# Attention reciprocals spread by GpSimd between two bias steps, and bias tables built a few steps a unit

## The chip, the cores and the metric

The kernel runs on one core of a Trainium2 chip. The core has engines with a queue each: TensorE (PE, matrix products and transposes into PSUM; its weight loads are listed as PEld), VectorE (DVE), ScalarE (ACT), GpSimd (POOL) and SyncE (SP, which issues DMAs). ACT and POOL issue DMAs too. Each engine takes its own instructions in order and waits on semaphores for the others. The metric is the time of one execution in microseconds on the device, lower is better. The time before is the median of three runs, 1032.79 us (1032.4 to 1032.83).

## The reference

One layer of a diffusion trunk: a modulated RMSNorm, a projection into a pooling mixer and into queries, keys and values, neighbourhood attention, an output projection with a gated residual, and a squared-ReLU MLP. The change lies in the neighbourhood attention. Its core, for one row of the 16 x 64 grid of tokens:

```python
s_loc = jnp.einsum('bnqhd,brnkhd->bhnqrk', q_r, k_b).astype(jnp.float32) * scale
bias = rpb[:, dr_idx[None, None, :, None], dc_idx]
s_loc = jnp.where(col_mask, s_loc + bias.astype(jnp.float32), -jnp.inf)
s_ctx = jnp.einsum('bnqhd,bkhd->bhnqk', q_r, k_ctx).astype(jnp.float32) * scale
s = jnp.concatenate([s_loc.reshape(B, H, NA_NCB, NA_QB, n_loc), s_ctx], axis=-1)
p = jax.nn.softmax(s, axis=-1).astype(v.dtype)
```

followed by the weighted sum of the values of the window and of the 256 context keys. There are 8 heads of 64 channels and 1024 queries.

## The kernel before

The kernel computes all of attention in float32. It cuts the 1024 queries into 8 tiles `m` of 128 (16 rows by 8 columns) and the 8 heads into 4 pairs `j`. One pair of heads on one tile is a **unit**; there are 32, numbered `i = 8j + m`. An inner unit has 640 keys a head (three tiles of the grid and the context), an edge unit (m = 0 or 7) 512.

The loop `for i in range(N + 4)` (L1160) is a software pipeline. In iteration i, besides other work:

- `scores(i)` (L969): PE multiplies queries and keys of both heads into two PSUM tiles `S` of two banks each, of which the pool holds two, so the next unit's scores of a head need the tile that this unit's bias step of that head has read. Then, for e = 0 and 1, DVE runs the **bias step** (L998): it adds the bias table `tab` to `S`, writes `sp` and takes the minimum `nm`.
- `turn(i-2)` (L1018): PE transposes, first the reciprocals `rb` of unit i-2 (into small areas of the banks `pa` and `pz`), then the probabilities `sp`. `fifth_kept` (ACT) and `turn_kept` (ACT for one half, DVE for the other, L1045) copy the results out of PSUM.
- `exps(i, e)` (L1003): ACT takes the exponential and its sum `su`.
- `share(i-1)` (L1009): DVE takes the reciprocal of the two sums (`ri`, 128 x 2) and copies it out to `rb` (128 x 128, each reciprocal 64 times), so that the transposes can turn it.
- `values(i-3)` (L1048): PE multiplies probabilities and values into `pa`.
- `weighed(i-4)` (L1065), at the head of the iteration: DVE multiplies `pa` by the turned reciprocals into `f` (L1070).

On PE the order in an iteration is scores, transposes, values. On DVE it is `weighed`, the two bias steps, the copy of the transposes, the reciprocal, the copy to `rb`.

**Tables.** `tables(j)` (L867) builds the bias tables of pair j: two DMAs on SP bring `U` (shifted rows of the bias), and twelve POOL instructions (L883), three for each head and each of two masks, subtract it from the mask into `tab`. There are two sets of table pages, used in turn. In the loop `tables(j+1)` is called as a whole in the iteration of m = 2.

**Order.** The orders of PE, ACT, DVE and SP in the loop are those of the program text (`in_order`, L104), and so is POOL's (`first_pool`, L1149). POOL's share of the loop before the change is: the table steps; adds by DMA (`add_to`, L187) in iterations 1 and 2 (`y<-y`), at i % 8 == 3 (`y<-f`, `ss<-f`, behind `weighed`), at i % 8 == 7 (`f<-ss`, which must wait for `ss<-f` to land) and at i = 32 (`to_0w`, `to_1w`); and three small reductions over the partitions for the modulation. Of these `mod_out` (L250) in iteration 4 writes a row to DRAM in four DMAs (`ga`); `column_sums` (L619) in iterations 5 (`sc`) and 8 (`sh`) does the same and then reads that row back by a further DMA on POOL's queue:

```python
def column_sums(name, acc, to, bank):
    nc.scalar.copy(acc[:, :256], mod_sums_of(name, acc, bank))
    mod_out(name, acc)
    nc.gpsimd.dma_start(to, gates[name].rearrange("o (k p) -> p (o k)", p=P))
```

In the text of an iteration these stand ahead of `scores(i)`.

Of the kernel before, what the change touches and what calls it, by code (L numbers as in the profile page):

```python
# [80 lines left out]
def hybrid_block(ctx, tc, x, ctx_in, w_mod, b_mod, gp1, gp2, w_in, pool_w, rpb, w_out, w1, w2, vectors,  # L81
                 mask, edge, out):
    nc = tc.nc
# [12 lines left out]
    def sm(name, n, bufs=1):  # L96
        return small.tile([P, n], F32, tag=name.split("_")[0], name=name, bufs=bufs)

    def page(name, dt=F32):
        return act.tile([P, 1024], dt, tag="pg", name=name)  # L100


    @contextmanager
    def in_order(*engines):  # L104
        block = nc.cur_bb
        n = len(block.bb.instructions)
        last = {}
        yield last
        assert nc.cur_bb is block
        for i in block.bb.instructions[n:]:  # L110
            if i.engine in engines:
                if i.engine in last:
                    tc.add_manual_dep(i, last[i.engine].name,
                                      mybir.DependencyInfo(mybir.DependencyClass.NoSync, mybir.DependencyReason.DATA),
                                      reason="order")
                last[i.engine] = i
# [154 lines left out]
    with tc.tile_pool(name="ps1", bufs=6, space=PSUM) as ps1, tc.tile_pool(name="tmp1", bufs=3) as tmp:  # L271

        def bank(name):
            if name[:2] == "pm" or name in ("pxt1_0", "pxt0_2", "pxt1_7", "pct2", "pct3"):
                return lasting(name)
            return ps1.tile([P, 512], F32, tag="mm", name=name)
# [488 lines left out]
        def token_raw(name):  # L765
            raw = [tmp.tile([P, 512], F32, tag="t", name=f"{name}r{i}", bufs=7) for i in range(4)]
            for i in range(4):
                nc.sync.dma_start(raw[i], stored[name][:, i])
            return raw

        def token_operand(name, raw):
            rows_of[name] = []
            for i in range(4):
                h = page(f"{name}h{i}", F32R)
                split(raw[i], h[:, :512], h[:, 512:])
                rows_of[name].append((h[:, :512], h[:, 512:]))
                yield
# [39 lines left out]
        def use(step):  # L817
            for _, put, i in islice(uses, len(plan[step + 1]) if step + 1 < len(plan) else 0):
                put(i)
                fetch()  # L820
# [46 lines left out]
        def tables(j):  # L867
            if j < 2:
                tabs.append([page(f"tab{j}{e}") for e in range(2)])
                for t in tabs[j]:  # L870
                    nc.gpsimd.memset(t[:, NLOC:NKEY], 0.0)
            u = wraw.tile([P, 1024], F32, tag="raw", name="U0w") if j == 0 else page(f"U{j}")
            u = u.rearrange("p (e t) -> p e t", e=2)
            for e in range(2):
                base = rpb.offset + (2 * j + e) * TR * TC
                nc.sync.dma_start(u[:, e, :ULEN], bass.AP(tensor=rpb.tensor, offset=base,
                                                                 ap=[[TC, QR], [1, QC], [1, ULEN]]))
            for e in range(2):
                uv = u[:, e, : QR * TC].rearrange("p (r c) -> p r c", c=TC)
                t = tabs[j % 2][e]  # L880
                for a, o in ((1, 0), (0, NKEY)):
                    for i in range(3):
                        nc.gpsimd.tensor_tensor(  # L883
                            t[:, o + i * P : o + (i + 1) * P].rearrange("p (r c) -> p r c", c=QC),
                            msk[0][:, a, i], uv[:, :, i * QC : (i + 1) * QC], sub)


        kT, qT = [None] * 4, [[None] * 2 for _ in range(4)]
# [36 lines left out]
        def half_product(name, of, j, banks):  # L925
            a, w = operand[name]
            seventh(banks[j], j, a, weights[w, of], name not in ("P2", "P3", "P4"))
# [3 lines left out]
        with in_order(ET.PE, ET.Pool, ET.Activation, ET.DVE, ET.SP) as pooling:  # L931
            banks = {of: [bank(f"p{of}{j}") for j in range(2)] for of in "KQ"}
            use(-1)
            for step, (n, of, j) in enumerate([(n, of, j) for n, of in products for j in range(2)]):
                half_product(n, of, j, banks[of])
                use(step)
                if step in (5, 9, 17):
                    name = {5: "S1", 9: "S4", 17: "S3"}[step]
                    parts = token_operand(name, sraw[name])
                if step in (5, 7, 9, 11, 17, 19):  # L940
                    next(parts)
                    next(parts)
                if step in (7, 11):
                    name = {7: "S4", 11: "S3"}[step]
                    sraw[name] = token_raw(name)
                if step == 14:
                    mask_page()
                if step == 20:
                    tables(0)
                if step in (21, 22):  # L950
                    for g in range(2):
                        pool_mixed(2 * (step - 21) + g)
                kept_product(n, of, j, banks[of][j])


    with (
# [5 lines left out]
        units = [(j, m) for j in range(4) for m in range(NM)]  # L962
        probs, least, sums, shares, turns, turned, fifths, heads = {}, {}, {}, {}, {}, {}, {}, {}
# [5 lines left out]
        def scores(i):  # L969
            j, m = units[i]  # L970
            inner = 0 < m < NM - 1
            n = NKEY if inner else 4 * P
            o = 1 if m == 0 else 0
            q = qT[j][m // 4]
            cols = slice((m % 4) * P, (m % 4 + 1) * P)
            heads = [slice(e * HD, (e + 1) * HD) for e in range(2)]
            S = [ps_s.tile([P, 1024], F32, tag="S", name=f"S{j}_{m}_{e}") for e in range(2)]
            if inner:
                parts = ((128, kT[j][:, (m - 1) * P : (m + 2) * P]), (512, kc[:, j, :]))
            else:  # L980
                parts = ((0, kc[:, j, :]), (256, kT[j][:, (m + o - 1) * P : (m + o + 1) * P]))
            for c0, keys in parts:
                for e, hs in enumerate(heads):
                    nc.tensor.matmul(S[e][:, c0 : c0 + keys.shape[1]], q[hs, cols], keys[hs], start=True, stop=True)  # L984
            halves = lambda a: a.rearrange("p (a b) -> p a b", a=2)
            for e in range(2):
                t = tabs[j % 2][e]
                sp = att.tile([P, NKEY], F32, tag="sp", name=f"sp{j}_{m}_{e}", bufs=6)[:, :n]
                if inner:
                    s, bt, to = S[e][:, 128:768], t[:, :NKEY], sp  # L990
                else:
                    s, to = halves(S[e][:, 0:512]), halves(sp)
                    if o:
                        bt = halves(t[:, 2 * P : 8 * P])[:, :, P:]
                    else:
                        bt = halves(t[:, NLOC : NLOC + 512])
                nm = sm(f"nm_{i}_{e}", 1, 6)
                nc.vector.tensor_tensor_reduce(out=to, in0=s, in1=bt, scale=1.0, scalar=BIG, op0=add, op1=ALU.min,  # L998
                                               accum_out=nm)
                probs[i, e] = sp  # L1000
                least[i, e] = nm

        def exps(i, e):  # L1003
            if e == 0:
# [2 lines left out]
            nc.scalar.activation(sp, sp, AF.Exp, bias=least[i, e], scale=-1.0, accum_out=sums[i][:, e : e + 1])  # L1007

        def share(i):  # L1009
            ri = sm(f"ri_{i}", 2, 2)  # L1010
            nc.vector.reciprocal(ri, sums[i])
            shares[i] = att.tile([P, P], F32, tag="ri", name=f"rb{i}", bufs=2)
            nc.vector.tensor_copy(shares[i].rearrange("p (e t) -> p e t", e=2),
                                  ri.rearrange("p (e o) -> p e o", o=1).to_broadcast([P, 2, HD]))


# [56 lines left out]
        N = len(units)  # L1073
# [78 lines left out]
        with in_order(ET.PE, ET.Activation, ET.DVE, ET.SP) as projected:  # L1152

            def last_query(n, j):
                half_product(n, "Q", j, last_queries)
                kept_product(n, "Q", j, last_queries[j])

            for j in range(2):
                last_query("P7", j)
            for i in range(N + 4):  # L1160
                if i < N and units[i][1] == 2 and units[i][0] < 3:
                    tables(units[i][0] + 1)
                if i in LOADS:
                    weight_load(0, kks[LOADS.index(i)])
                if i == N:
# [44 lines left out]
                else:  # L1210

                    t = i - N
# [17 lines left out]
                    turn_kept(i - 2, 1, nc.vector.tensor_copy)  # L1230
                if i < 2:
                    last_query("P4", i)
                if 0 < i <= N:
                    share(i - 1)
                if 2 < i <= N + 2:
                    values(i - 3)
# [754 lines left out]
```

## Time and profile before

| | |
|---|---|
| median of 3 runs | 1032.79 us |
| profiled execution, its own span | 1030.8 us |
| attention stage in it | 218.8 to 322.4 us |
| DMA in it | 222.68 MB, mean 216 GB/s |

The profile is of one execution. Its page gives the busy time of each engine (share of the span, number of instructions), and the chain of work that ended last, followed back from the end, by engine. Other views list the instructions in order of time (start, duration, engine, line, operation, `out<-in`, shapes, count, and in brackets the idle time before and what ended it); who waited for whom (total us, times, longest); groups of instructions by line (busy us, mean ns of one, idle before); DMA issues (KB each, median us from issue to landing); and the busy time of PE, PEld, DVE, ACT and POOL in a stretch, followed by the granted TensorE clock (1.00 is full), the DMA share and GB/s. Ends of matmuls are modelled.

### The profile page before, as it was taken

How to read it: one execution, taken by the hardware profiler on the slowest of the kernel's cores; microseconds unless marked ns; L12 is line 12 of the kernel's file. 1: busy time of each engine (PE TensorE's matmuls, PEld its weight loads, DVE VectorE, ACT ScalarE, POOL GpSimd, SP SyncE). 2: the span in 40 equal slices, each digit the busy share in tenths (PEclk: the TensorE clock that was granted, in tenths of full speed). 3: DMA queues.
4: the chain of work that ended last, by engine and by line, in shares of the span. 5: the costliest groups of instructions: out<-in, count | busy, mean ns of one | idle time of the engine just before them, and what ended most of it. 6: DMA issues, size and time to landing. Idle time of an engine off the chain costs nothing.

```text
span 1030.8 us, 15588 instructions
## 1 busy us (share of the span) xinstructions
PE 1017.8 (99%) x5782; PEld 834.2 (81%) x5782; DVE 751.8 (73%) x1187; ACT 543.7 (53%) x941; POOL 110.7 (11%) x168
## 2 busy tenths in 40 slices
PE   8999999999999999999999999999999999999997
PEld 6788888877887888888888888888888888888885
DVE  5588767858996587878998887855766666547576
ACT  7573255328887556776655544555543334334431
POOL 3011200244311311310000000000000000000001
PEclk9999999999999999999999999999999999999999
DMA  9999798632337866795786666637967766555556
GB/s 343 332 255 338 246 265 296 204 86 80 72 95 194 203 180 200 253 237 168 267 269 210 204 210 214 205 122 241 327 220 271 248 226 220 202 180 189 176 182 211
DMA packets 123132, 222.68 MB, mean 216 GB/s; under 512 B 9456, under 2 KB 55152, under 8 KB 123056
## 3 DMA queue, kind: packets, MB, share of 16 engines
q1 hardware_dynamic: 96560, 171.14, 50.4%
q0 software_dynamic: 9360, 19.58, 9.5%
q10 hardware_dynamic: 17136, 30.97, 8.0%
q8 instruction: 45, 0.74, 0.3%
q14 instruction: 31, 0.25, 0.1%
HBM read 168.16 MB, written 52.45 MB: 214 GB/s over the span
## 4 chain that ended last, share of the span: by engine, by line
PE 95%; DMA 2%; ACT 1%; DVE 1%; issue 0%; SPq 0%; DVEq 0%; POOLq 0%; ACTq 0%
PE pu L449 4%; PE S L984 4%; PE pa L1060 3%; PE phv L198 3%; PE phz L198 3%; PE phx L198 3%; PE pyx L198 3%; PE phx L200 3%; PE phv L199 3%; PE phx L199 3%; PE pyx L199 3%; PE pyx L200 3%; PE pyv L199 3%; PE pyv L198 3%; PE pyz L199 3%; PE pyz L198 3%
## 5 line engine op out<-in xcount | busy, mean ns | idle before, releaser
L1007 ACT ACTIVATE sp<-sp,nm 128x640 f32<-128x640 f32 (+1 forms) x64 | 51.4, 803 | 20.0 <-DVE nm L998 19.6
L1577 ACT ACTIVATE c<-c 128x512 f32<-128x512 f32 x48 | 30.3, 632 | 47.0 <-DVE c L1697 28.2
L146 ACT CAST wpS<-S 128x512 fp32r<-128x512 f32 x64 | 38.7, 616 | 26.4 <-PE phv L200 9.2
L198 PE MATMUL phx<-thB,wpA 128*128 128x512 f32 x128 | 50.2, 392 | 0.0
L200 PE MATMUL phx<-thB,wpA 128*128 128x512 f32 x128 | 49.8, 389 | 0.0
L199 PE MATMUL phx<-tlB,wpA 128*128 128x512 f32 x128 | 49.8, 389 | 0.0
L152 DVE TENSOR_TENSOR wpS<-S,wpS 128x512 fp32r<-128x512 f32 x64 | 43.4, 685 | 8.3 <-ACT wpS L146 8.3
L998 DVE CUSTOM_DVE_ANT_0 sp<-S,tab 128x640 f32<-128x640 f32 (+1 forms) x56 | 42.9, 803 | 8.8 <-PE S L984 7.3
L1578 ACT ACTIVATE c<-c 128x512 f32<-128x512 f32 x48 | 30.3, 631 | 15.1 <-DVE sa L1660 12.3
L140 POOL TENSOR_TENSOR ry<-vy,nhalf 128x1 f32<-128x1 f32 x8 | 5.9, 740 | 280.7 <-DVE vy L138 280.7
L198 PEld LDWEIGHTS phx<-thB,wpA 128*128 128x128 f32 x128 | 24.0, 188 | 5.5 <-ACT s L1628 0.5
L984 PE MATMUL S<-kT,q 64*128 64x384 f32 (+1 forms) x128 | 27.9, 495 | 0.3 <-DVE nm L998 0.3
L200 PEld LDWEIGHTS phx<-thB,wpA 128*128 128x128 f32 x128 | 24.0, 188 | 5.0
L199 PEld LDWEIGHTS phx<-tlB,wpA 128*128 128x128 f32 x128 | 24.0, 188 | 4.9
L1060 PE MATMUL pa<-pt,v 128*64 128x128 f32 x352 | 25.9, 279 | 0.6 <-ACT px L1040 0.2
L1045 DVE COPY pt<-T 128x512 f32<-128x512 f32 x32 | 22.0, 686 | 5.5 <-PE T L1026 5.5
L198 PE MATMUL phv<-thT,wpA 128*128 128x512 f32 x64 | 25.1, 392 | 0.0
L198 PE MATMUL phz<-thB,wpS 128*128 128x512 f32 x64 | 25.0, 391 | 0.0
L200 PE MATMUL phv<-thT,wpA 128*128 128x512 f32 x64 | 24.9, 389 | 0.0
L199 PE MATMUL phv<-tlT,wpA 128*128 128x512 f32 x64 | 24.9, 389 | 0.0
L200 PE MATMUL phz<-thB,wpS 128*128 128x512 f32 x64 | 24.9, 389 | 0.0
L199 PE MATMUL phz<-tlB,wpS 128*128 128x512 f32 x64 | 24.9, 389 | 0.0
(1100 smaller groups left out, 3359.7 us busy)
## 6 DMA issues: line engine op xcount, KB each, us to landing
b<-in_w SPq DMA_DIRECT2D x64, 512.0 KB, 4.2
hrS<-hdS SPq DMA_DIRECT2D x32, 512.0 KB, 5.1
hrA<-hdA SPq DMA_DIRECT2D x24, 512.0 KB, 5.5
wm<-in_w_mod SPq DMA_DIRECT2D x16, 512.0 KB, 9.7
wa_0w<-in_w SPq DMA_DIRECT2D x16, 512.0 KB, 5.3
wa_1w<-in_w SPq DMA_DIRECT2D x16, 512.0 KB, 4.5
hdA<-c ACTq DMA_DIRECT2D x32, 256.0 KB, 2.8
hdS<-sa ACTq DMA_DIRECT2D x32, 256.0 KB, 2.7
```

The source lines that it names most:

```text
L146: nc.scalar.copy(hi, src)
L152: nc.vector.tensor_tensor(lo, src, hi.bitcast(F32), sub)
L198: nc.tensor.matmul(ps, ahi, bhi, start=first, stop=False, skip_group_check=more)
L199: nc.tensor.matmul(ps, ahi, blo, start=False, stop=False, skip_group_check=more)
L200: nc.tensor.matmul(ps, alo, bhi, start=False, stop=last, skip_group_check=more)
L449: nc.tensor.matmul(pus[b][j], wk(wgt, k, low, j * P, P), r, start=(k == 0 and n == 0), stop=(k == KT - 1 and n == 2))
L984: nc.tensor.matmul(S[e][:, c0 : c0 + keys.shape[1]], q[hs, cols], keys[hs], start=True, stop=True)
L998: nc.vector.tensor_tensor_reduce(out=to, in0=s, in1=bt, scale=1.0, scalar=BIG, op0=add, op1=ALU.min, accum_out=nm)
L1007: nc.scalar.activation(sp, sp, AF.Exp, bias=least[i, e], scale=-1.0, accum_out=sums[i][:, e : e + 1])
L1060: nc.tensor.matmul(pa[e * HD : (e + 1) * HD, cols], v[:, f : f + HD], turns[i][:, e, c] if c < 4 else fifths[i][:, :, (e + 1) * HD : (e + ...
L1577: nc.scalar.activation(r, src, AF.Relu)
L1578: nc.scalar.activation(r, r, AF.Square)
```

## The change

The copy of the reciprocals to `rb` goes from DVE to POOL. The reciprocal and this copy of unit i-1 are issued inside `scores(i)`, between the two bias steps of unit i, instead of near the end of iteration i; only the last unit's stay at the old place. `ri` gets three buffers instead of two. `tables` becomes a generator: its first step (pages, fills, the DMAs of U) runs in the iteration of m = 1, and then three POOL instructions follow in each of the iterations of m = 2 to 5. The tables of the first pair, ahead of the loop, are still built at one go.

```diff
@@ tables(j)
                 nc.sync.dma_start(u[:, e, :ULEN], bass.AP(tensor=rpb.tensor, offset=base,
                                                                  ap=[[TC, QR], [1, QC], [1, ULEN]]))
+            yield
             for e in range(2):
...
                             msk[0][:, a, i], uv[:, :, i * QC : (i + 1) * QC], sub)
+                    yield
@@ ahead of the loop
                 if step == 20:
-                    tables(0)
+                    for _ in tables(0):
+                        pass
@@ scores(i), after the bias step of head e
                 least[i, e] = nm
+                if e == 0 and i > 0:
+                    share(i - 1)
@@ share(i)
-            ri = sm(f"ri_{i}", 2, 2)
+            ri = sm(f"ri_{i}", 2, 3)
             nc.vector.reciprocal(ri, sums[i])
             shares[i] = att.tile([P, P], F32, tag="ri", name=f"rb{i}", bufs=2)
-            nc.vector.tensor_copy(shares[i].rearrange("p (e t) -> p e t", e=2),
+            nc.gpsimd.tensor_copy(shares[i].rearrange("p (e t) -> p e t", e=2),
                                   ri.rearrange("p (e o) -> p e o", o=1).to_broadcast([P, 2, HD]))
@@ the loop
+            coming_tables = iter(())
             for i in range(N + 4):
-                if i < N and units[i][1] == 2 and units[i][0] < 3:
-                    tables(units[i][0] + 1)
+                if i < N and units[i][1] == 1 and units[i][0] < 3:
+                    coming_tables = tables(units[i][0] + 1)
+                next(coming_tables, None)
...
-                if 0 < i <= N:
+                if i == N:
                     share(i - 1)
```

## The prediction

> **What bounds the kernel now.** I read the page from the top: busy times, then the chain that ended last, then, for the attention stage where all edits lie, the stretch's busy times.
>
> ```profile
> span 1030.8 us, 15588 instructions
> PE 1017.8 (99%) x5782; PEld 834.2 (81%) x5782; DVE 751.8 (73%) x1187; ACT 543.7 (53%) x941; POOL 110.7 (11%) x168
> ...
> PE 95%; DMA 2%; ACT 1%; DVE 1%; issue 0%; SPq 0%; DVEq 0%; POOLq 0%; ACTq 0%
> ```
>
> ```profile
> 218.80:322.40 103.60, 102.88 (x1490) 81.71 (x1489) 87.88 (x258) 85.11 (x225) 34.92 (x63) 1.00 0.44 111
> ```
>
> PE is 95% of the chain, and in the attention stage (218.8 to 322.4) it is busy for 102.88 of 103.6 us, against DVE's 87.88. Its ends are modelled, so I check one unit in the timeline: unit 6, whose scores begin at 240.58.
>
> ```profile
> 240.58 0.30 PEld L984 LDWEIGHTS S<-kT,q 64*128 64x128 f32 x4 [0.17 <-DVE nm L998]
> ...
> 241.33 0.60 PE L984 MATMUL S<-kcT,q 64*128 64x256 f32 x4
> 241.54 0.14 PEld L1026 LDWEIGHTS pa<-ident,rb 64*128 64x128 f32 x1
> ...
> 241.96 0.82 DVE L998 CUSTOM_DVE_ANT_0 sp<-S,tab 128x640 f32<-128x640 f32 x1 [0.48 <-PE S L984]
> ...
> 242.71 0.82 DVE L998 CUSTOM_DVE_ANT_0 sp<-S,tab 128x640 f32<-128x640 f32 x1
> ...
> 243.45 0.08 DVE L998 DVE_READ_ACCUMULATOR2_ANT nm<- 128x1 f32 x1
> 243.45 0.69 DVE L1045 COPY pt<-T 128x512 f32<-128x512 f32 x1
> ...
> 243.77 0.30 PEld L984 LDWEIGHTS S<-kcT,q 64*128 64x128 f32 x4 [0.17 <-issue]
> ...
> 244.05 0.15 DVE L1011 RECIPROCAL ri<-su 128x2 f32<-128x2 f32 x1
> ...
> 244.24 0.23 DVE L1013 COPY rb<-ri 128x128 f32<-128x128 f32 x1
> 244.38 0.28 DVE L1070 TENSOR_TENSOR f<-pa,px 128x128 f32<-128x128 f32 x1
> ...
> 244.72 0.14 PEld L1026 LDWEIGHTS pa<-ident,rb 64*128 64x128 f32 x1 [0.22 <-DVE f L1070]
> ```
>
> The unit lasts 243.77 - 240.58 = 3.19 us. PE goes scores, transposes (the one of rb first), values, next scores, with a pause of 0.17 that has no releaser. DVE stands idle 0.48 for S. So PE sets the pace. DVE is what PE sometimes waits for, in a small sum:
>
> ```profile
> PEld S L984 <- DVE nm L998: 2.4, 11, 0.5
> ...
> PEld pa L1026 <- DVE f L1070: 1.6, 7, 0.4
> ```
>
> **The change, part by part.** (a) *The copy leaves DVE*: 0.23 us a unit for 31 of 32 units, as L1013's row has it. DVE has slack in a steady unit, so the saving reaches PE only where the transposes wait for f (L1070): at most 1.6 us.
>
> (b) *The reciprocal moves between the two bias steps.* The second one ends 0.15 later (L1011). The next unit's scores of head 1 reuse the bank it reads. It now ends with its accumulator read at 243.45 + 0.08 = 243.53; PE starts the next scores at 243.77. With 0.15 it is 243.68, still inside, so the price is nothing; the cover is PE's own values, and without that cover it is 0.15 a unit. Where units are shorter than this one (after an edge unit, which has fewer keys) the bank is late already, and there part of (a) is given back. Bounds for (a) and (b) together: a gain of 1.6, a loss of 0.15 x 11 = 1.7 (the 11 waits on nm). I take a gain of 0.5: the 0.15 fits in most units, and of seven waits for f I let about a third go.
>
> (c) *The copy on POOL.* It is not in this trace. The nearest POOL rows, by size, are two at 128x128, a fill-like select and the two-input table step:
>
> ```profile
> masks.py:199 POOL TENSOR_SCALAR_AFFINE_SELECT ident<-ident 128x128 f32<-128x128 f32 x1 | 0.3, 288 | 0.0
> L883 POOL TENSOR_TENSOR tab<-msk,U 128x128 f32<-128x128 f32 x36 | 15.3, 459 | 17.2 <-DMA U<-in_rpb 17.2
> ```
>
> I take 0.28 (one input, as the select), bounds 0.2 and 0.46, and 0.06 for the signal to PE. The reciprocal now ends near 242.71 + 0.15 and rb is wanted at 244.72, behind the next unit's scores. So by itself the copy is hidden, with over 1 us to spare.
>
> (d) *What stands ahead of it on POOL.* This is the part that decides. POOL's order in the loop is written out, so each copy stands behind everything that its iteration puts on POOL before the scores, the DMAs with their waits included:
>
> ```profile
> 238.68 1.91 POOL L253 DMA_DIRECT2D gsc<-accsc  x4 [2.17 <-ACT accsc L621]
> 242.22 0.93 POOL L623 DMA_DIRECT2D sc<-gsc  x1 [1.63 <-DMA gsc<-accsc]
> 248.28 1.95 POOL L253 DMA_DIRECT2D gsh<-accsh  x4 [5.14 <-ACT accsh L621]
> 253.14 0.92 POOL L623 DMA_DIRECT2D s<-gsh  x1 [2.91 <-DMA gsh<-accsh]
> 254.08 4.94 POOL L883 TENSOR_TENSOR tab<-msk,U 128x128 f32<-128x128 f32 x12
> ```
>
> `column_sums` (iterations 5 and 8) sends a row to DRAM and reads it back, and POOL stands still until the row has landed. That the queue really holds later work is in the last row: the table steps of iteration 10 begin at 254.08, just as the DMA of iteration 8 ends, though their U was issued at 244.98 and lands in 3.8:
>
> ```profile
> 244.98 1.25 SPq L876 DMA_DIRECT2D U<-in_rpb  x2
> ```
>
> ```profile
> U<-in_rpb SPq DMA_DIRECT2D x2, 244.5 KB, 3.8
> ```
>
> Today nobody waits for POOL there. After the change rb of unit 4 comes behind the sc DMA (242.22 + 0.93 = 243.15) and rb of unit 7 behind the sh DMA (253.14 + 0.92 = 254.06). Unit 4's transposes stand at 241.54 today, unit 7's here:
>
> ```profile
> 251.32 0.14 PEld L1026 LDWEIGHTS pa<-ident,rb 64*128 64x128 f32 x1
> ```
>
> So PE stands for 243.15 + 0.02 + 0.28 + 0.06 - 241.54 = 1.97 us in iteration 6, and 254.06 + 0.36 - 251.32 = 3.10 us in iteration 9: 5.07 us. PE takes its queue in order, so values and the next scores move by as much, and the stage has no slack to win it back.
>
> (e) *The rest of POOL's queue*:
>
> ```profile
> 308.07 0.85 POOL L188 DMA_DIRECT2D y<-f  x1 [17.59 <-DVE f L1070]
> 308.61 1.19 POOL L188 DMA_DIRECT2D ss<-f  x1
> 317.33 0.86 POOL L188 DMA_DIRECT2D f<-ss  x1 [7.54 <-DMA ss<-f]
> 317.87 1.57 POOL L188 DMA_DIRECT2D to_0w<-in_w_out  x1
> 318.58 2.10 POOL L188 DMA_DIRECT2D to_1w<-in_w_out  x1
> ```
>
> ```profile
> to_1w<-in_w_out POOLq DMA_DIRECT2D x1, 512.0 KB, 13.1
> ```
>
> ```profile
> L146 ACT CAST to_0h<-to_0w x1: 1052/1052/1052, 340.6 to 340.6; 128x1024 fp32r<-128x1024 f32 x1
> ```
>
> At i = 11, 19, 27 two adds stand ahead of the copy: f is ready 0.9 us into the unit (244.66 against 243.77), their issue takes 309.80 - 308.07 = 1.73, the copy 0.34, so rb is there after 3.0; it is wanted after 4.1 (3.19 + 0.95). The table steps, three a unit, take 3 x 0.44 = 1.3 us behind the previous copy: hidden. U is issued one unit sooner and must now be there at m = 2; by the rows above it lands some 4 us before POOL could begin. The tables are whole three units ahead of their first use. The ss<-f wait now stands four units behind its issue, and the longest landing (317.33 - 308.61 = 8.7 us) is shorter than four units (12.8). The adds to t1 (317.87, 318.58) go behind the last copies, about 4 us later; at 13.1 to landing the second is there near 336, and its first reader comes after 340.6. All of (e): nothing, with a loss of 0.5 us as the bound.
>
> (f) *PE's clock.* A pause of PE can cost more than its length. The granted clock at the start and the end of the run:
>
> ```profile
> 1.60:5.20 3.60, 3.60 (x17) 3.60 (x18) 0.35 (x4) 1.21 (x3) 0.00 (x0) 1.00 0.89 306
> 5.20:6.90 1.70, 1.65 (x15) 1.41 (x13) 0.86 (x6) 1.70 (x3) 0.53 (x1) 1.00 1.03 422
> 1020.00:1023.60 3.60, 3.57 (x16) 2.63 (x14) 1.12 (x1) 0.00 (x0) 0.00 (x0) 1.00 0.66 171
> 1023.60:1025.80 2.20, 0.00 (x0) 0.00 (x0) 1.35 (x3) 0.69 (x2) 0.55 (x1) 1.00 0.30 119
> 1025.80:1030.80 5.00, 0.00 (x0) 0.00 (x0) 0.83 (x2) 0.00 (x0) 0.00 (x0) 0.50 0.35 105
> ```
>
> The clock (third number from the right) falls to 0.50 some 2.2 us after the last matmul. At the start 17 matmuls take 3.60 us (0.21 each) and then 15 take 1.65 (0.11 each): half speed for 3.6 us of work before the full one. In iteration 6 PE is empty from about 241.93 (241.33 + 0.60) to 243.51, 1.6 us: under 2.2, the clock stays. In iteration 9 it is empty as far behind the transposes' place (241.93 - 241.54 = 0.39), from 251.71 to 254.42, 2.7 us: over 2.2, so I count one stretch at half clock, which does in 3.6 us the work of 1.8 and costs about 1.7; bounds 0 and 3.6 (both pauses).
>
> The Trainium skill ("TensorE: Matmul & The Clock Gate", section "Part 1: The HAM clock gate (the "warmup" mystery)") asks for a whole idle window of about 3.4 us before the clock is halved, in windows that run freely. By that neither pause is long enough and the sum goes without this term. The trace halved after 2.2 us, which differs, so the row decides here.
>
> **The sum**: -0.5 + 1.97 + 3.10 + 1.7 = +6.3 us. Against the profiled execution's span, 1030.8 + 6.3 = 1037.1; the median of the runs shown, 1032.79, lies 2.0 above that span, so 1039.1.
>
> **Rivals.**
> 1. *The pauses come, the clock stays*: the sum without (f), +4.6, 1037.4. For it: 2.7 us is not much over the 2.2 that were seen, once, at the end of the run. Against it: that one case. The rule of the Trainium skill quoted in (f) speaks for it as well.
> 2. *Both pauses halve the clock*: +8.0, 1040.8. The first pause is 0.6 us short of the 2.2.
> 3. *The bank of head 1 sets the next scores*, if its release needs more than the 0.09 us that (b) leaves (243.77 - 243.68): up to 0.15 in each of 24 inner units, 3.6 on top of the forecast, 1042.7. Against it: the pause ahead of the scores is 0.17 with and without nm as its releaser.
> 4. *Faster: DVE, not PE, paces the stage*, PE's busy time being modelled. Then each unit is shorter by the whole copy, 32 x 0.23 = 7.3 us, against the pauses of 5.1: -2.2, 1030.6. It decides if DVE has no real idle time; against it are the 0.48 us idle before L998 and 87.88 of 103.6.
> 5. *The copies aren't held by the DMA waits* (the change's own order differs from what I read): only the 0.5 of (a), 1032.3, at best 1031.2. Against it: the 254.08 row.
>
> **How the numbers follow.** Forecast 0.43, rival 1 0.28, rival 2 0.11, rival 3 0.06, rival 4 0.06, rival 5 0.06. The range holds the forecast, rivals 1 and 2 (0.82): from rival 1 with the full gain of (a) and (b), 1.1 less, and a landing half a us sooner, 1035.8, to rival 2 with half a us for (e), 1041.3. A measurement of this kernel tells about 0.2% (2.1 us) from no change. Slower by more: the forecast and rivals 1 to 3, 0.88, and a bit is taken off for landings that come much sooner than here: 0.87. Rival 4 and the better end of rival 5 are faster, 0.07; the rest, 0.06, is the same.
>
> **What would show it.** Right: in the changed profile PE's transposes wait for the rb copy on POOL, about 2.0 and 3.1 us, in two units, nowhere else for long; the two copies start at the end of the sc and s reads; the waits for f are below 1.6; the granted clock dips once, after the second pause. Rival 3 shows as S waiting for nm in most units, rival 4 as units below 3.19 us. Wrong altogether: copies that start right after their reciprocal while the sc read is still waiting.

## The result, and the profile after

The changed kernel takes 1037.57 us (median of 5 runs, 1036.74 to 1038.1) against 1032.62 (1032.09 to 1032.83) for the kernel before on the same chip: a ratio of 1.0047, 95% interval 1.0034 to 1.0059. It is 4.95 us slower, inside the forecast range and 1.5 us under the forecast. It lies close to the first rival's number (1037.4): the pauses came, the half clock did not. How far that number was luck is said further down.

The head of the page of the changed kernel:

```profile
span 1035.6 us, 15717 instructions
PE 1018.5 (98%) x5782; PEld 836.1 (81%) x5782; DVE 745.2 (72%) x1155; ACT 544.3 (53%) x941; POOL 120.8 (12%) x200
```

DVE lost 6.6 us of work, POOL gained 10, and PE's work is the same while its share fell: PE waits. For what, the view of waits over the attention stage says (total us, times, longest):

```profile
PEld pa L1031 <- POOL rb L1018: 4.5, 2, 2.4
...
PE pa L1031 <- POOL rb L1018: 3.7, 2, 2.0
```

Two waits of the transposes for rb (PEld and PE list the same two). Before, the waits for f (L1070, now L1075) were seven and made 1.6 us; they are gone from this list, and PE pays two long ones in their place. Where they lie shows in POOL's instructions in order of time:

```profile
239.09 1.95 POOL L253 DMA_DIRECT2D gsc<-accsc  x4 [0.64 <-ACT accsc L621]
242.67 0.94 POOL L623 DMA_DIRECT2D sc<-gsc  x1 [1.63 <-PE S L987]
243.60 0.53 POOL L1018 COPY rb<-ri 128x128 f32<-128x128 f32 x2
...
250.54 1.93 POOL L253 DMA_DIRECT2D gsh<-accsh  x4 [2.12 <-ACT accsh L621]
254.67 0.93 POOL L623 DMA_DIRECT2D s<-gsh  x1 [2.19 <-DMA gsh<-accsh]
255.59 0.53 POOL L1018 COPY rb<-ri 128x128 f32<-128x128 f32 x2
```

Each time the copy starts in the moment in which the read-back's issue ends (242.67 + 0.94; 254.67 + 0.93), and two copies come out together: the late one and the next unit's, which was ready too. (The first wait is put down to PE S by the view; the read follows its row's landing, as in the kernel before, where the idle time was 1.63 as well and the view named the DMA.) PE in iterations 6 and 9:

```profile
240.98 0.30 PEld L987 LDWEIGHTS S<-kT,q 64*128 64x128 f32 x4 [0.17 <-DVE nm L1001]
...
243.96 0.14 PEld L1031 LDWEIGHTS pa<-ident,rb 64*128 64x128 f32 x1 [2.03 <-POOL rb L1018]
```

```profile
252.57 0.30 PEld L987 LDWEIGHTS S<-kT,q 64*128 64x128 f32 x4 [0.17 <-issue]
...
255.94 0.14 PEld L1031 LDWEIGHTS pa<-ident,rb 64*128 64x128 f32 x1 [2.43 <-POOL rb L1018]
```

Without the wait the transposes follow the scores by 0.97 (251.32 against 250.35 before). So the places of the transposes are 240.98 + 0.97 = 241.95 and 252.57 + 0.97 = 253.54, and PE lost 243.96 - 241.95 = 2.0 us and 255.94 - 253.54 = 2.4.

To compare all runs I use one length, called the **loop** below: from the first weight load of unit 0's scores to that of unit 31's, read from the instruction list of each profile. It was 319.27 - 218.83 = 100.44 us before and is 323.51 - 219.18 = 104.33 now, 3.9 more. Units 6 and 9 grew by 1.85 and 2.25 (3.20 to 5.05; 3.07 to 5.32), the other 29 periods together shrank by 0.2. Of the 4.8 us between the two spans the remaining 0.9 lie outside the loop, 0.35 ahead of it and 0.5 behind; they come up again below.

### The profile page after: what moved, and what is told of

Read it like the earlier page. It is cut to its first block, busy times and chain, and to the rows that moved or that the text cites. A ratio compares the mean times of both kernels' runs of the same rounds, so it can differ in the third digit from the quotient of the medians.

```text
span 1035.6 us, 15717 instructions
## 1 busy us (share of the span) xinstructions
PE 1018.5 (98%) x5782; PEld 836.1 (81%) x5782; DVE 745.2 (72%) x1155; ACT 544.3 (53%) x941; POOL 120.8 (12%) x200
## 4 chain that ended last, share of the span: by engine, by line
PE 93%; DMA 3%; ACT 2%; issue 1%; DVE 1%; SPq 0%; POOL 0%; POOLq 0%; DVEq 0%; ACTq 0%
PE pu L449 4%; PE S L987 3%; PE pa L1065 3%; PE phz L198 3%; PE phv L198 3%; PE phx L198 3%; PE pyx L198 3%; PE pyv L200 3%; PE phz L199 3%; PE phv L199 3%; PE pyz L200 3%; PE phx L199 3%; PE phx L200 3%; PE pyx L200 3%; PE pyv L198 3%; PE pyz L198 3%
## 5 line engine op out<-in xcount | busy, mean ns | idle before, releaser
L198 PE MATMUL phz<-thB,wpS 128*128 128x512 f32 x64 | 25.0, 391 | 0.0
L198 PE MATMUL phy<-thT,wpS 128*128 128x512 f32 x64 | 24.9, 389 | 0.0
```

Source lines behind the costliest of these rows:

```text
L198: nc.tensor.matmul(ps, ahi, bhi, start=first, stop=False, skip_group_check=more)
```

## The experiments

My theory: each copy waits on POOL's queue for the DMA waits ahead of it, and this is all of the loss. The rivals: the place between the bias steps costs in every unit; POOL and DVE get in each other's way; the tables in steps cost something.

### The read-backs moved away

```diff
 def column_sums(name, acc, to, bank):
     nc.scalar.copy(acc[:, :256], mod_sums_of(name, acc, bank))
     mod_out(name, acc)
-    nc.gpsimd.dma_start(to, gates[name].rearrange("o (k p) -> p (o k)", p=P))
+
+def read_back(name, to):
+    nc.gpsimd.dma_start(to, gates[name].rearrange("o (k p) -> p (o k)", p=P))
@@ the loop
+                if i == 7:
+                    read_back("sc", scale2)
+                if i == 10:
+                    read_back("sh", s2)
```

> The changed kernel, but the two DMAs on POOL that read the reduced rows back (sc, sh) are issued two iterations later (7 and 10), when their rows have long landed. Theory (copies held behind DMA waits): the transposes' two waits for rb, 2.0 and 2.4 us, go, so 1037.6 - 4.1 = 1033.5 us; if the 0.8 us that PE loses near 360 us also comes from the stalls, 1032.7. Rival (the bank of head 1, or port sharing between POOL and DVE, costs a little in every unit): the time stays above 1036.5.

Measured: 1033.03 us against 1033.03 before on that chip, ratio 0.9999 (0.9991 to 1.0008); loop 100.24. POOL's instructions in this run:

```profile
239.26 1.96 POOL L253 DMA_DIRECT2D gsc<-accsc  x4 [0.64 <-ACT accsc L621]
241.21 0.30 POOL L1020 COPY rb<-ri 128x128 f32<-128x128 f32 x1
243.60 0.29 POOL L1020 COPY rb<-ri 128x128 f32<-128x128 f32 x1 [2.09 <-DVE ri L1018]
244.25 0.94 POOL L625 DMA_DIRECT2D sc<-gsc  x1 [0.35 <-issue]
```

The copy now comes right behind the writes, in time, and the read finds its row landed. No wait of the transposes for rb is left among the stage's waits. The two read-backs are the whole loss in the loop (104.33 - 100.24 = 4.1). What is left of the change's gain is 0.2 us of loop, which the median can't show.

### The tables alone, and the copy given back to DVE

The first puts the stepwise tables into the kernel before, with nothing else. The second is the changed kernel with one word changed:

```diff
-            nc.gpsimd.tensor_copy(shares[i].rearrange("p (e t) -> p e t", e=2),
+            nc.vector.tensor_copy(shares[i].rearrange("p (e t) -> p e t", e=2),
```

> The kernel before with the stepwise tables alone; reciprocal and copy stay on DVE at their old place. Theory: nothing waits for POOL or for the tables, so 1032.6 us, within 0.2%. Rival (the spread steps disturb DVE's two-input work or the loads): 0.5 us or more slower.

> The changed kernel, but the copy to rb is DVE's again, still between the two bias steps; POOL no longer touches rb. Theory: the two stalls go (4.1 us), and the second bias step now ends 0.06 + 0.23 = 0.29 us later than before the change, against 0.24 us of room before the next scores: up to 0.1 us a unit in 24 units, 1033 to 1035.5 us. Rival (what costs is the place between the bias steps, not POOL): 1037 or more.

Both were misses. The tables alone cost 1035.3 us against 1033.03, ratio 1.0023 (1.0014 to 1.0033), loop 102.89. The copy on DVE costs 1039.28, ratio 1.0071 (1.0055 to 1.0087), loop 106.17: the slowest version apart from the longer pause with fills below. Its time fell where the rival had put it, but the rival's cause is not shown by that: the place alone costs 1.6 us (only_between, below). The copy's own durations show the rest (ns, min/median/max), in the tables-alone kernel and in the copy-on-DVE kernel:

```profile
L1016 DVE COPY rb<-ri x32: 226/227/1851, 228.9 to 330.4; 128x128 f32<-128x128 f32 x32
```

```profile
L1018 DVE COPY rb<-ri x32: 226/228/2847, 225.9 to 333.5; 128x128 f32<-128x128 f32 x32
```

Before, the longest was 392 ns. POOL and DVE around the longest copy of the copy-on-DVE kernel:

```profile
285.00 1.16 POOL L188 DMA_DIRECT2D ss<-f  x1
285.56 3.06 POOL L884 TENSOR_TENSOR tab<-msk,U 128x128 f32<-128x128 f32 x6
```

```profile
285.47 2.85 DVE L1018 COPY rb<-ri 128x128 f32<-128x128 f32 x1
288.24 0.81 DVE L1001 CUSTOM_DVE_ANT_0 sp<-S,tab 128x640 f32<-128x640 f32 x1
```

The copy hangs until the table steps that were queued behind the adds by DMA are nearly through, and the second bias step, the bank of head 1 and PE hang with it: unit 20 takes 7.51 us instead of 3.47. Part of that is a half clock of PE behind this pause, from 289.31 to 292.72 (last section). With the copy on DVE nothing on POOL paces the steps, so six of them run in a row right behind the adds of m = 3. In the kernel before, all twelve stood ahead of those adds. The next run puts this order back, still in steps.

### The steps ahead of the adds

```diff
                 next(coming_tables, None)
+                if i < N and units[i][1] in (2, 3):
+                    next(coming_tables, None)
```

> As only_tables (DVE keeps the copy at its old place), but the twelve steps go six and six into the iterations of m = 2 and 3, so that all of them stand ahead of the adds by DMA of m = 3 and none right behind. Theory (table steps queued right behind the adds keep the port that POOL and DVE's copy share, so DVE's copy took 1.85 us instead of 0.23, twice): both long copies are gone and the time is the kernel's before, 1033.0. Rival (cutting the tables into steps costs as such): 1035.3 as only_tables.

Measured: 1032.61 against 1032.69, ratio 0.9998 (0.9989 to 1.0007), loop 100.40, and the copy's row is the old one again:

```profile
L1016 DVE COPY rb<-ri x32: 226/227/404, 228.1 to 327.0; 128x128 f32<-128x128 f32 x32
```

So steps as such cost nothing; steps queued right behind an add by DMA cost DVE's copy 1.6 us, twice (1.85 and 1.78 instead of 0.23).

### The place between the bias steps alone

The kernel before with `share` called between the bias steps, copy on DVE, tables as before.

> The kernel before with reciprocal and copy between the two bias steps, both on DVE; tables at one go at m = 2 as before. It prices the place. Theory: the second bias step ends 0.34 us later (3.29 instead of 2.95 after the scores' start, as in copy_on_dve), the bank of head 1 is late by about 0.1 us, inner units take 3.26 to 3.34 instead of 3.20: 1 to 2 us over before, 1034 to 1035 us. Rival (the place costs nothing, all of copy_on_dve's loss was blocked copies): 1033.0.

Measured: 1034.47, ratio 1.0017 (1.0008 to 1.0027), loop 102.07: 1.6 more, as expected. Its DVE row shows no long copy:

```profile
L1015 DVE COPY rb<-ri x32: 226/227/391, 225.6 to 329.0; 128x128 f32<-128x128 f32 x32
```

The second bias step now ends 3.29 us after its unit's scores began instead of 2.96 (medians of the inner units), which uses up the 0.24 us that it had before the next scores. In the list of instructions units 10, 18 and 26 last 3.12 instead of 2.86 to 2.93, and the inner ones 6, 28 and 30 last 3.33 to 3.34 instead of 3.20; in these three the next scores begin within 0.05 us of the step's end. So the bank of head 1 is what they wait for. With the copy on POOL the step ends after 3.02 us and 0.18 us are left: the place is cheap only because the copy left DVE with it.

### The tables at one go, with the copy on POOL

As in the first experiment, with `tables` called as a whole at m = 2.

> As later_reads, but the tables are again built at one go in the iteration of m = 2. Theory: twelve steps (4.9 us) stand ahead of one copy three times, in iterations 2, 10 and 18; the copy comes about 0.4, 0.9 and 1.5 us late, so 2 to 3 us over later_reads, 1035 to 1036.5 us, with three waits of the transposes for rb. Rival (compute work on POOL does not hold the copy for long, only DMA waits do): the same as later_reads.

Measured: 1037.77, ratio 1.0043 (1.0027 to 1.0058), loop 105.47: the three waits are there, but the version is 4.7 us over later_reads, more than the 2 to 3 expected. By the view of waits the transposes' three make 4.4 us, the longest 1.8. POOL in the first of the three places:

```profile
225.45 0.29 POOL L1020 COPY rb<-ri 128x128 f32<-128x128 f32 x1 [14.95 <-DVE ri L1018]
225.68 0.56 POOL L873 MEMSET tab<- 128x256 f32 x2
226.21 4.93 POOL L886 TENSOR_TENSOR tab<-msk,U 128x128 f32<-128x128 f32 x12
231.09 1.65 POOL L188 DMA_DIRECT2D y<-y  x2
232.22 1.05 POOL L1020 COPY rb<-ri 128x128 f32<-128x128 f32 x2
```

I had counted the twelve steps and forgotten what else stands there: the fills, and the two adds of iteration 2 (1.65 us); in iteration 10 it was the moved read-back (0.94). And behind the pause of iteration 3 PE ran at half clock for 3.41 us (last section), which costs about 1.7 us; that is an estimate, half of the 3.41. With the copy on POOL the steps are needed.

### Longer pauses, for the clock

The changed kernel with fills on POOL between the sh read-back and the copy: five in the first run, thirteen in the second.

```diff
                     column_sums("sh", accs["sh"], s2, rest_of_bank)
+                    filler = att.tile([P, 256], F32, tag="gp", name="filler")
+                    for _ in range(5):
+                        nc.gpsimd.memset(filler, 0.0)
```

> The changed kernel with five fills (128x256, 0.26 us apart, about 1.3 us) on POOL between the sh row's read-back and the copy of unit 7's reciprocals, so that PE's empty time in iteration 9 grows from 2.0 to about 3.3 us. If the clock halves after 2.2 us without matmuls (the row at the end of the run): granted clock 0.5 for some 3.5 us after the pause, 1.3 + 1.7 = 3.0 us over the changed kernel, 1040.6 us. If it takes a whole idle window of 3.4 us: clock stays 1.00, 1.3 us over, 1038.9 us.

> The same with thirteen fills (about 3.4 us), PE empty for about 5.4 us. Both readings of the clock say it halves: 3.4 + 1.7 = 5.1 us over the changed kernel, 1042.7 us, with a stretch of granted clock 0.5. If pauses of this size never halve it: 1041.0 us.

One execution each: 1038.82 and 1042.29 us. The fills took some 0.36 us each (five in 1.80), not 0.26, so the pauses were longer than planned. Stretches of the first run, then of the second (length, busy PE, PEld, DVE, ACT, POOL, then granted clock, DMA share, GB/s):

```profile
254.15:257.67 3.52, 0.00 (x1) 0.00 (x1) 1.64 (x5) 0.00 (x0) 2.79 (x8) 1.00 0.12 6
252.54:255.95 3.41, 1.61 (x15) 0.78 (x10) 2.98 (x8) 1.24 (x4) 1.41 (x3) 1.00 0.03 5
255.96:259.37 3.41, 1.70 (x36) 1.64 (x38) 0.69 (x1) 1.39 (x5) 2.95 (x9) 1.00 0.10 1
```

```profile
253.56:256.97 3.41, 0.19 (x2) 0.00 (x0) 1.64 (x5) 0.00 (x0) 2.49 (x6) 1.00 0.11 6
256.98:260.39 3.41, 0.18 (x4) 0.18 (x6) 0.00 (x0) 0.00 (x0) 2.96 (x11) 0.50 0.00 0
260.39:263.80 3.41, 3.41 (x40) 2.96 (x39) 0.69 (x1) 2.44 (x7) 1.23 (x3) 0.50 0.01 2
263.81:267.22 3.41, 3.41 (x45) 2.79 (x47) 2.40 (x7) 1.51 (x5) 1.04 (x3) 1.00 0.00 0
```

PE stood empty for 3.52 us and kept its clock; 2.2 us at the end of the kernel before had halved it. In the second run the empty time (253.75 to 260.21) halved it at 256.98, and it came back at 263.80. Read as a length of the pause, neither 2.2 nor 3.4 us decides: 3.52 us are longer than both. The last section says what fits better.

### The splits of the output weights in quarters

In the first experiment's kernel the units 12, 14, 20 and 22 last 3.34 to 3.35 us, where ACT carries a 0.6 us split of the output weights. I cut these splits into quarters of 256 columns and spread them:

```diff
-        LOADS, HALVES = (8, 16, 26, 28), (12, 14, 20, 22, 32, 33, 33, 34)
+        LOADS, QUARTERS = (8, 16, 26, 28), (11, 12, 13, 14, 19, 20, 21, 22, 32, 32, 33, 33, 33, 33, 34, 34)
```

> later_reads, with ACT's and DVE's splits of the output weights cut from 512 to 256 columns and spread over units 11 to 14 and 19 to 22 (two units longer in all lists). Theory: in later_reads the units 12, 14, 20 and 22, which carry a 0.6 us split on ACT, last 3.34 instead of 3.20; 0.35 fits into ACT's 0.45 us of idle time a unit, so the loop is 0.5 us shorter than later_reads (99.7 us from first to last scores), median 1032.5, hardly to be told from 1033.0. Rival (these units are long for another reason): loop of 100.2 us.

Measured: loop 99.77, as expected, with units 12, 14, 20 and 22 at 3.20. The median is 1032.05 against 1032.69, ratio 0.9994 (0.9985 to 1.0003): the shortest time of all versions, but its interval holds 1, so that it is faster than the kernel before isn't shown. Not all of the 0.5 us of loop belongs to the change either: units 14 and 22 took 3.34 in the kernel before, too. Quarters without the rest of the change were not run.

## Why the prediction was right, and where not

- **(d) What stands ahead on POOL** was right in cause, place and sign; later_reads shows it. The first pause was 2.0 us (1.97 forecast), the second 2.4 (3.10): there POOL waited 2.19 us for the sh row instead of 2.91, the one term of (d) that was mis-sized.
- **(c) The copy** takes 0.29 us (0.28 forecast), and up to 0.93 right behind the adds, still in time.
- **(f) The clock** is the step that failed. It put 1.7 us on the second pause because the trace before halved the clock 2.2 us after the last matmul. After the change the granted clock stayed 1.00 through both pauses. PE was without a matmul for 1.63 and 2.03 us in them (the rows above give the weight loads' 2.03 and 2.43), where 1.6 and 2.7 were forecast; the sh row landed sooner. Both lie under the 2.2, so this result alone would still fit the forecast's reading. What refutes it is pause_1: 3.52 us empty at a full clock. I had read one row as a threshold in length; it isn't one.
- **(a) and (b) The gain** was 0.2 us in the loop instead of 0.5. The reciprocal delays the second bias step by 0.06, not by its whole 0.15, since it overlaps the step before it, and unit 11 is indeed shorter (3.31 to 3.19). But unit 12 is longer (3.25 to 3.35): with DVE out of the way ACT's split is next, and the gain goes there. quarter_splits, where unit 12 takes 3.20, shows that this was the bound.
- **(e) The rest of POOL's queue** cost nothing in the loop, as put. Outside the loop it stays open. Behind the loop the changed profile lost 0.5 us, by the chain at DMAs into `to_3w`: from the first matmul of `poz` to the last matmul of the kernel it takes 673.53 us against 672.93 before. With the copy on DVE the five profiles (before, only_tables, copy_on_dve, steps_before_adds, only_between) take 672.76 to 672.99 us there. With the copy on POOL the changed kernel, later_reads, tables_whole and quarter_splits take 673.16 to 673.53, but pause_1 and pause_3, also on POOL, 672.83 and 672.62. That is one profile each; whether the change costs some 0.4 us there was not tested by itself. The 0.35 us ahead of the loop I count as scatter: the code there is the same, and over all profiles the loop's start lies between 218.83 and 219.77.
- **Rival 3** (the bank of head 1) is real, but not here: with the copy on DVE it costs 1.6 us, with the copy on POOL there is room. **Rival 4** falls: relieved of 0.23 us a unit DVE made units no shorter than PE allows. **Rival 5** falls with the two rows of copies that start where the read-backs end.

The sum by the measured terms: 1.85 + 2.25 - 0.2 = 3.9 us in the loop and 0.9 outside it make the 4.8 of the two spans; the medians differ by 4.95. So it is partly luck that rival 1's 4.6 comes so close. Its terms stand for the loop alone, where 3.9 were measured: the two pauses lengthened their units by 4.1 us instead of 5.07, and the gain was 0.3 smaller than put. The 0.9 outside the loop, for which no term of the sum stands, fill the gap.

## What to carry to other kernels

Before work goes to an engine that stands idle, list what is already in its queue, waits included: an engine busy for 11% of the time was blocked for 2 us at two places, and that became the price. A wait that nobody waits for is free until something urgent is queued behind it; here moving two small reads by two iterations gave all of it back. And check the part that looks like a mere rearrangement by itself: the stepwise tables cost nothing, or 2.3 us, depending on which instruction stands just ahead of them.

## What the runs showed of the hardware

**The clock is judged in fixed windows.** In tables_whole the granted clock was low from 234.15 to 237.56, 3.41 us, in pause_3 for twice that. The windows just before and during a half clock, of tables_whole, of copy_on_dve and of the end of the kernel before:

```profile
230.74:234.15 3.41, 2.04 (x32) 1.36 (x30) 1.92 (x7) 1.65 (x6) 2.53 (x5) 1.00 0.53 90
234.15:237.56 3.41, 3.41 (x28) 1.97 (x26) 1.32 (x3) 2.03 (x5) 0.00 (x0) 0.50 0.75 204
```

```profile
285.90:289.31 3.41, 1.56 (x14) 0.77 (x12) 3.41 (x4) 1.10 (x4) 2.73 (x7) 1.00 0.89 151
289.31:292.72 3.41, 3.41 (x30) 2.52 (x30) 2.48 (x9) 2.28 (x6) 0.90 (x1) 0.50 0.10 18
```

```profile
1022.43:1025.84 3.41, 1.14 (x6) 0.60 (x4) 1.39 (x3) 0.69 (x2) 0.55 (x1) 1.00 0.54 143
1025.84:1030.80 4.96, 0.00 (x0) 0.00 (x0) 0.79 (x2) 0.00 (x0) 0.00 (x0) 0.50 0.35 106
```

Counted from the clock's first change in each profile, all later changes lie on multiples of 3.413 us. That is the grid of windows used here and above; in tables_whole the first change is at 5.46 and the other two lie 67 and 68 windows later. A window with 1.56 us of (modelled) PE work halved the clock, and one with 2.04; in pause_1 two windows in a row with 1.61 and 1.70 did not, though PE stood empty for 3.52 us across them. So the length of a pause alone does not decide, and where it falls among the windows matters. The share of PE work in a window fits part of it. At the runs' ends, where the work is the same, windows with a share of 0.30 to 0.37 halved the clock (before, changed, only_tables, quarter_splits) and one with 0.43 did not (pause_3). In the attention stage 0.06 (pause_3) and 0.46 (copy_on_dve) halved it, while 0.47 and 0.50 (pause_1) and 0.49 and 0.52 (changed) did not. The halving at 2.04 / 3.41 = 0.60 does not fit; whether the modelled ends of the matmuls explain it stays open. The Trainium skill ("TensorE: Matmul & The Clock Gate", section "Part 1: The HAM clock gate (the "warmup" mystery)") gives a freely running window of 3413 ns, and the traces agree; that a whole window must be idle, as it says, they do not bear out (1.14 us of PE work in the window that halved the clock at the end of the kernel before).

**A DVE copy can be shut out by POOL for far longer than one POOL instruction.** Beside table steps alone the 0.23 us copy took 0.43 at most; beside steps queued behind an add by DMA it took 1.78 and 1.85 (only_tables), 1.13 and 2.85 (copy_on_dve). One copy in copy_on_dve, at 260.06, started 0.2 us ahead of such steps and took 0.23. The Trainium skill ("SBUF — State Buffer", section "Who interferes with whom") says that POOL and a DVE copy within SBUF can need the same pair of ports, and that whoever issues first has it for a whole instruction. That would make a block of one table step, about 0.44 us. The traces show a block, but of several steps. One thing differs in their records: a step mostly takes 0.44 us, but about 1.0 to 1.1 us right behind an add, while one still starts every 0.41 us, so that the records of neighbouring steps overlap. Whether this is what keeps the copy out, and why the DMA ahead causes it, was not tested.
